# Three longer visits to the gate's projection in a chunk of the recurrence, in place of six

## The chip, the cores and the metric

The kernel runs on one core of a Trainium2 chip. The metric is the device time of one execution in microseconds (us), the median of some runs. A core has TensorE for matmuls (PE in the profile, and PEld for its weight loads), VectorE (DVE), ScalarE (ACT), GpSimd (POOL) and SyncE (SP), which here only issues transfers. Each engine works through its own instructions in the order in which they are written, and they meet at semaphores. TensorE writes into PSUM, eight banks from which VectorE and ScalarE carry the results away.

## The reference

One step of a decoder trunk with two layers over 1024 prompt tokens and 8 sample tokens: first an RWKV-7 layer with 32 heads of 64, then a latent attention layer. The change is in the RWKV-7 layer, in the recurrence over the prompt and the output that is made of it:

```
r, k, v, z = einsum('pbtd,pde->pbte', mixed, w_in)
...
def _wkv_step(S, inp):
    r, w, k, v, a, b = inp
    sa = einsum('bhvk,bhk->bhv', S, a)
    S = S * w[:, :, None, :] + sa[..., None] * b[:, :, None, :] + v[..., None] * k[:, :, None, :]
    return S, einsum('bhvk,bhk->bhv', S, r)
...
yn = ((y - mu) * rsqrt(var + GN_EPS)) * lnx_w + lnx_b      # per head
bonus = sum(rh * kh * r_k) * vh
out = ((yn + bonus) * silu(z)) @ w_out
```

The projection z is the gate's; nothing in the recurrence needs it.

## The kernel before, in words

The recurrence (`phase_r`, line 1208 on) takes the 1024 tokens in 32 chunks of 32, `for c in range(NC)`. The 32 heads are two groups g of 16. In a chunk each group goes through four small steps, and each is 16 to 32 short matmuls on TensorE into one PSUM bank and a copy out of it:

- `rh(c, g)` (line 1257): the right-hand side from the state; ScalarE copies it out as `rhs` (L1265).
- `sa(c, g)` (line 1267): the solve, with the inverse in tile U; ScalarE and VectorE each copy two quarters into the state tile st (L1276).
- `new_state(c, g)` (line 1278): the next state, named s in the trace; VectorE multiplies it with the decay into the other state tile in two instructions (L1289).
- `outs(c, g)` (line 1292): the chunk's output y, four copies by ScalarE (L1305).

rh needs the product of the state behind new_state of the chunk before, sa needs rhs, new_state needs the copies behind sa, and rh of the next chunk also needs the rows of v that `loadv` (line 1249) puts into the state tile; it is issued by SyncE and overwrites rows that outs(c - 1, 1) still reads. The loads of a later chunk's tiles X (xz) and U are issued beside it.

Between the small steps TensorE works on the gate's projection: `fill(w)` (line 1466) takes a number of steps of the generator zg, which is w times `rate` on average. A step is three matmuls of 128x344, named p in the trace; 333 steps are left when the loop starts, and `rate` (line 1461) spreads them over the chunks but for the last. Here this is called a visit. In the last chunk the output projection's generator opg takes their place.

The loop has six pieces a chunk, i = 0 to 5: rh of group 0; new_state of group 1 of the chunk before; sa of group 0 with outs of group 1 of the chunk before, and the loads; rh of group 1; new_state of group 0; sa of group 1 with outs of group 0. Behind each piece comes one step of the output block's generator ob, one step of the sample tokens' generator sg (a single-token recurrence on GpSimd and VectorE), and a visit with weight 0.8, or 1.4 behind the third and the sixth piece.

ob is `out_block(B)` (line 1432), started every four chunks for the outputs of the last four. It normalises them in two halves; each half is `out_half` (line 1315), with 18 steps, and the second half starts six steps after the first, so the block has 24 steps, as many as four chunks have pieces. Of a half, steps 0 and 1 and steps 7 and 8 are a reduce and its scale on VectorE, steps 9, 10, 14 and 15 are products on VectorE, steps 5 and 6 squares on ScalarE. Steps 16 and 17 each transpose half of the half on TensorE, four matmuls named ot (L1365), into the bank `tr`, of which there is one, and ScalarE copies it out as ozt (L1366). So step 17's transposes can start only when step 16's copy has ended. Step 17 also stores ozt.

Nothing plans the order: every engine gets its instructions in the order in which the loop and its generators issue them.

Of the kernel before, what the change touches and what calls it, by code (L numbers as in the profile page):

```python
# [31 lines left out]
NC = S // C  # L32
# [23 lines left out]
def tile_yoco(ctx, tc, A, O, dbg=None):  # L56
# [4 lines left out]
    def mm(out, lhsT, rhs, start, stop):  # L61
        PE.matmul(out, lhsT=lhsT, rhs=rhs, start=start, stop=stop)  # L62
# [97 lines left out]
    def run(g):  # L160
        for _ in g:
            pass

    def chain(*gs):
        for g in gs:
            yield from g
# [1041 lines left out]
    def phase_r(mh, ml, gC, bon, osT, SM, zg, zbank, zx):  # L1208

        with ExitStack() as px:  # L1210
# [9 lines left out]
            def psum(tag, name, bufs):  # L1220
                return ps.tile([P, 512], F32, tag=tag, name=name, bufs=bufs)

            def units(X):
                for s_ in range(2):
                    rows = slice(64 * s_, 64 * s_ + 64)
                    ACT.copy(X[rows, :, ts(2 * s_, 64)],
                             ident[rows, 64 * s_:64 * s_ + 64].unsqueeze(1).to_broadcast([64, 16, 64]))
# [3 lines left out]
            def load(c):  # L1231
                if c >= NC:
                    return
                X = XZ[c % NX]
                for s_ in range(2):
                    rows = slice(64 * s_, 64 * s_ + 64)
                    SY.dma_start(X[rows, :, 128 - 128 * s_:256 - 128 * s_], xs_d[s_, c].rearrange("r (a t) -> r a t", t=P))
                    (ACT if c > 2 else SY).dma_start(X[rows, :, 64 + 128 * s_:128 + 128 * s_], ra_d[:, rows, c].rearrange("a r t -> r a t"))
# [10 lines left out]
            def loadv(c):  # L1249
                if c < NC:  # L1250
                    SY.dma_start(ST[0][c % 2][96:128], v_d[0, ts(c, 32)])
                    SY.dma_start(ST[1][c % 2][32:64], v_d[1, ts(c, 32)])
# [4 lines left out]
            def rh(c, g):  # L1257
                X = XZ[c % NX]
                pr = psum("rh", f"rh{c}_{g}", 1)
                p3 = pr[:, 0:256].rearrange("p (q d) -> p q d", d=64)  # L1260
                for h in range(16 * g, 16 * g + 16):
                    j, q, s_ = h % 4, h // 4 - 4 * g, h % 2
                    mm(p3[ts(j, 32), q, :], X[:, h // 2, 128 * s_ + 96:128 * s_ + 128], ST[s_][c % 2][:, h // 2, :], True, True)
                t_ = rhs[g] = w1.tile([P, 4, 64], F32, tag=f"rh{g}", name=f"rhs{c}_{g}")
                ACT.copy(t_.rearrange("p q d -> p (q d)"), pr[:, 0:256])  # L1265

            def sa(c, g):
                U = Us[c]
                pa = [psum(f"sa{u}", f"sa{c}_{g}{u}", 1)[:, 0:256].rearrange("p (q d) -> p q d", d=64) for u in range(2)]
                for h in range(16 * g, 16 * g + 16):  # L1270
                    j, q = h % 4, h // 4 - 4 * g
                    mm(pa[j % 2][ts(j, 32), q, :], U[ts(j, 32), 4 * g + q, :], rhs[g][ts(j, 32), q, :], True, True)
                for j in range(4):
                    t_ = ST[0][c % 2][64:96] if j % 2 == 0 else ST[1][c % 2][0:32]
                    d = t_.rearrange("p (q two) d -> p q two d", two=2)[:, 4 * g:4 * g + 4, j // 2, :]
                    (V.tensor_copy if j % 2 else ACT.copy)(d, pa[j % 2][ts(j, 32)])  # L1276

            def new_state(c, g):

                X = XZ[c % NX]  # L1280
                p3 = psum("sy0", f"s{c}_{g}", 1).rearrange("p (q d) -> p q d", d=64)
                for q in range(8):
                    for s_ in range(2):
                        a = 8 * g + q
                        mm(p3[ts(s_, 64), q, :], X[:, a, 128 * s_:128 * s_ + 64], ST[s_][c % 2][:, a, :], True, True)
                qs = slice(8 * g, 8 * g + 8)
                for s_ in range(2):
                    rows = slice(64 * s_, 64 * s_ + 64)
                    V.tensor_tensor(ST[s_][1 - c % 2][rows, qs, :], p3[rows],  # L1289
                                    gC[rows, qs, c:c + 1].to_broadcast([64, 8, 64]), ALU.mult)  # L1290

            def outs(c, g):

                X = XZ[c % NX]
                B, ci = divmod(c, 4)
                if B not in ys:
                    ys[B] = w2.tile([P, 16, 2, 64], F32, tag="y", name=f"y{B}")
                p_ = psum("sy1", f"y{c}_{g}", 1)
                for m in range(4):
                    for j in range(4):  # L1300
                        a, s_ = 8 * g + 2 * j + m // 2, m % 2
                        mm(p_[ts(j, 32), ts(m, 64)], X[:, a, 128 * s_ + 64:128 * s_ + 96], ST[s_][c % 2][:, a, :], True, True)
                for j in range(4):
                    a = 8 * g + 2 * j
                    ACT.copy(ys[B][ts(ci, 32), a:a + 2].rearrange("p a s d -> p (a s d)"), p_[ts(j, 32), 0:256])  # L1305
# [126 lines left out]
            def out_block(B, lag=6):  # L1432
                a, b = out_half(B, 0), out_half(B, 1)
                n = 0
                while a is not None or b is not None:
                    if a is not None and next(a, end) is end:
                        a = None
                    if n >= lag and b is not None and next(b, end) is end:
                        b = None
                    n += 1  # L1440
                    yield
# [5 lines left out]
            sg = sample_step(sp, lambda n: psum("tr", n, 1), osT, SM)  # L1447
# [16 lines left out]
            ob = chain()  # L1464

            def fill(w):
                nonlocal due
                due += w * rate
                while due >= 1.0:
                    next(zg, None)  # L1470
                    due -= 1.0

            for c in range(NC):
                for i in range(6):
                    if i == 0:
                        rh(c, 0)
                    elif i == 1:
                        if c:
                            new_state(c - 1, 1)
                            if c % 4 == 0:  # L1480
                                run(ob)
                                ob = out_block(c // 4 - 1)
                        if c == NC - 1:
                            run(sg)
                            run(zg)
                            rx.close()
                            zx.close()
                            opg = op_open()
                    elif i == 2:
                        sa(c, 0)  # L1490
                        if c:
                            outs(c - 1, 1)
                        loadv(c + 1)
                        load(c + 2)
                        loadu(c + 2)
                        if c == 2:
                            SY.dma_start(lnw, A["a_lnx_w"].to_broadcast([P, DI]))
                        if c == 0:
                            for X in XZ[1:]:
                                units(X)  # L1500
                    elif i == 3:
                        rh(c, 1)
                    elif i == 4:
                        new_state(c, 0)
                    else:
                        sa(c, 1)
                        outs(c, 0)
                    next(ob, None)
                    next(sg, None)
                    fill(1.4 if i % 3 == 2 else 0.8)  # L1510
                    if c == NC - 1 and i in (1, 5):
                        next(opg)
            new_state(NC - 1, 1)
            outs(NC - 1, 1)
# [14 lines left out]
            ob = out_last(NC // 4 - 1)  # L1529
# [44 lines left out]
    def op_open():  # L1574
        rp = rsx.enter_context(tc.tile_pool(name="rsp", bufs=1, side="right", reuse_waits="tile"))
        mid["RS"] = rp.tile([P, T], F32, name="RS")

        for nm, sh in (("cks", [P, 2, NB]), ("kps", [64, NB]), ("ckn", [NB, KVL]),
                       ("qsp", [64, HB, NB]), ("zsb", [P, HB, NB])):
            mid[nm] = rp.tile(sh, F32, name=nm)  # L1580
        mid["idx"] = rp.tile([P, NB, 8], I32, name="idx")
        wx = mid["wx"] = ExitStack()
        wA = wx.enter_context(tc.tile_pool(name="wA", bufs=1, side="right", reuse_waits="tile"))
        mid["op"] = a_out(wx, wA)
        return mid["op"]
# [1187 lines left out]
```

## Time and profile before

| | us |
|---|---|
| median of 3 runs | 2931.27 (2929.74 to 2937.22) |
| the profiled execution, its own time | 2943.64 |
| its span, first to last instruction | 2941.9 |
| TensorE busy in the span | 2696.3 (92%) |
| VectorE busy | 1672.7 (57%) |
| ScalarE busy | 1361.2 (46%) |
| GpSimd busy | 1430.5 (49%) |

The busy shares are means over the whole program. The recurrence is the stretch from about 990 to 1484 us of the span. A row of the timeline gives the start and the length of an instruction or of several merged ones (xcount); in the brackets at its end stands how long the engine was idle before it and what ended that. "issue" means that nothing in the profile shows what it waited for. PEclk is the granted clock of TensorE as a share of its full 2.4 GHz. A matmul's end is modelled, so matmuls that follow each other overlap in the rows; the distance of two starts is what they cost.

### The profile page before, as it was taken

To read this page: it belongs to the slowest core of one execution; us is meant where nothing else is said; L and a number is where in the kernel's file an instruction comes from. 1 tells how busy PE (TensorE), PEld (TensorE's weight loads), DVE (VectorE), ACT (ScalarE), POOL (GpSimd) and SP (SyncE) were. 2 spreads that over 40 slices of the span, in tenths; PEclk is the share of its full clock that TensorE was granted. 3 is DMA by queue.
4 is the path that set the end of the run, shared out by engine and by line. 5 is a ranking of instruction groups with operands and counts; after the bars stand their busy time and mean duration, and the time that the engine had idled before them with its cause. 6 is when DMAs were issued, how large, how long until landed. Compare 5 with 4: busy or idle time off the path is not lost.

```text
span 2941.9 us, 64866 instructions
## 1 busy us (share of the span) xinstructions
PE 2696.3 (92%) x26386; PEld 2418.5 (82%) x26386; DVE 1672.7 (57%) x2952; ACT 1361.2 (46%) x2886; POOL 1430.5 (49%) x1385
## 2 busy tenths in 40 slices
PE   7999998878786788888879999999999999899998
PEld 7999997766675677767769989999999999666897
DVE  7232117989797756666574144127777777533414
ACT  7232226767675444445454335225555555333423
POOL 3322121699999566663245455313444433475342
PEclk9999999989898899999989999999999999999999
DMA  4332334667677899999777552322111111586525
GB/s 157 120 126 76 96 88 113 162 145 174 155 162 190 206 223 218 227 227 210 175 228 225 173 123 78 107 83 83 54 56 54 56 52 55 157 274 201 179 90 187
DMA packets 567501, 423.80 MB, mean 144 GB/s; under 512 B 176260, under 2 KB 515649, under 8 KB 567074
## 3 DMA queue, kind: packets, MB, share of 16 engines
q1 hardware_dynamic: 473954, 336.06, 42.5%
q10 hardware_dynamic: 79648, 38.42, 4.9%
q0 software_dynamic: 13600, 45.16, 4.9%
q8 instruction: 208, 3.41, 0.5%
q14 instruction: 91, 0.75, 0.1%
HBM read 281.69 MB, written 133.35 MB: 141 GB/s over the span
## 4 chain that ended last, share of the span: by engine, by line
PE 57%; POOL 7%; DVE 7%; DMA 5%; issue 4%; ACT 3%; SPq 1%; ACTq 0%; DVEq 0%; POOLq 0%
PE p L62 8%; PE zb L62 6%; PE sc L62 6%; PE bo L62 5%; PE wop L62 4%; PE o L62 4%; POOL Xt L1081 2%; POOL X L1083 2%; PE s L62 2%; PE q L62 2%; PE pt L2156 2%; PE v L62 2%; PE k L62 1%; PE pt L2575 1%; PE bt L62 1%
## 5 line engine op out<-in xcount | busy, mean ns | idle before, releaser
L76 POOL TENSOR_TENSOR wl<-wr,wh 128x1024 fp32r<-128x1024 f32 x32 | 84.3, 2654 | 288.0 <-ACT wh L71 269.5
L1081 POOL TENSOR_TENSOR Xt<-N,X 128x31 f32<-128x31 f32 (+15 forms) x217 | 187.0, 862 | 27.2 <-DMA N<-n_d 11.0
L1083 POOL TENSOR_TENSOR X<-X,Xt 128x31 f32<-128x31 f32 (+15 forms) x217 | 183.8, 847 | 17.0
L71 ACT CAST pth<-pt 128x256 fp32r<-128x256 f32 (+1 forms) x320 | 108.2, 355 | 128.8 <-DVE ptl L76 74.8
L1289 DVE TENSOR_TENSOR st<-s,gC 64x512 f32<-64x512 f32 x128 | 88.2, 689 | 131.6 <-PE s L62 129.2
L62 PE MATMUL p<-mh,w3h 128*128 128x344 f32 x384 | 149.6, 390 | 6.2 <-issue 5.0
L76 DVE TENSOR_TENSOR ptl<-pt,pth 128x256 fp32r<-128x256 f32 (+1 forms) x320 | 120.9, 391 | 27.0 <-ACT pth L71 25.0
L62 PE MATMUL p<-ml,w3h 128*128 128x344 f32 x384 | 130.8, 341 | 5.1 <-issue 2.9
L62 PE MATMUL p<-mh,w1h 128*128 128x344 f32 x360 | 134.9, 375 | 0.0
L62 PE MATMUL p<-mh,w3l 128*128 128x344 f32 x384 | 127.1, 337 | 3.7 <-issue 3.7
L62 PE MATMUL r<-mh,wh 128*128 128x344 f32 x384 | 124.7, 325 | 4.6 <-ACT tf L483 4.6
L62 PE MATMUL r<-mh,wl 128*128 128x344 f32 x384 | 124.1, 323 | 0.0
L62 PE MATMUL r<-ml,wh 128*128 128x344 f32 x384 | 123.9, 323 | 0.0
L2139 ACT ACTIVATE pr<-sc,mx 128x128 f32<-128x128 f32 (+7 forms) x128 | 95.4, 745 | 53.1 <-DVE mx L2136 51.6
L62 PE MATMUL p<-mh,w1l 128*128 128x344 f32 x360 | 119.9, 333 | 0.0
L62 PE MATMUL p<-ml,w1h 128*128 128x344 f32 x360 | 119.8, 333 | 0.0
L2136 DVE TENSOR_REDUCE mx<-sc 128x1 f32<-128x128 f32 (+7 forms) x128 | 96.7, 755 | 3.2
L1305 ACT COPY y<-y 32x256 f32<-32x256 f32 x256 | 93.2, 364 | 10.7 <-PE y L62 7.1
L1276 ACT COPY st<-sa 32x256 f32<-32x256 f32 x128 | 46.4, 362 | 111.1 <-PE sa L62 100.7
L1950 DVE TENSOR_TENSOR zbr<-zb,RS 128x384 f32<-128x384 f32 (+1 forms) x48 | 24.6, 515 | 126.1 <-PE zb L62 123.8
L62 PEld LDWEIGHTS s<-st,xz 128*64 128x64 f32 x2048 | 72.6, 148 | 27.9 <-issue 20.9
L2041 POOL TENSOR_TENSOR qp<-qp,rope 128x256 f32<-128x256 f32 (+1 forms) x30 | 22.4, 747 | 145.8 <-DMA qsw<-qp 122.4
(1237 smaller groups left out, 9944.9 us busy)
## 6 DMA issues: line engine op xcount, KB each, us to landing
xs_d<-XS SPq DMA_DIRECT2D x64, 512.0 KB, 5.9
xz<-xs_d SPq DMA_DIRECT2D x64, 512.0 KB, 9.0
wr<-in_a_w_in_dram SPq DMA_DIRECT2D x17, 1024.0 KB, 6.1
ra_d<-RA SPq DMA_DIRECT2D x32, 512.0 KB, 7.3
xz<-ra_d ACTq DMA_DIRECT2D x58, 256.0 KB, 7.4
rT_d<-rr ACTq DMA_DIRECT2D x16, 516.0 KB, 2.6
R<-rT_d SPq DMA_DIRECT2D x16, 516.0 KB, 3.5
w3r<-in_a_w_in_dram SPq DMA_DIRECT2D x16, 512.0 KB, 6.2
```

Source lines behind the costliest of these rows:

```text
L62: PE.matmul(out, lhsT=lhsT, rhs=rhs, start=start, stop=stop)
L71: ACT.copy(out, in_)
L76: (eng or V).tensor_tensor(out, in_, hi_.bitcast(F32), ALU.subtract)
L1081: eng.tensor_tensor(t3, N_[:, s_:s_ + 1, s_ + 1:].to_broadcast([P, a, b]), X_[:, r0:r1, s_:s_ + 1].to_broadcast([P, a, b]), ALU.mult)
L1083: eng.tensor_tensor(X_[:, r0:r1, s_ + 1:], X_[:, r0:r1, s_ + 1:], t3, ALU.add)
L1276: (V.tensor_copy if j % 2 else ACT.copy)(d, pa[j % 2][ts(j, 32)])
L1289: V.tensor_tensor(ST[s_][1 - c % 2][rows, qs, :], p3[rows], gC[rows, qs, c:c + 1].to_broadcast([64, 8, 64]), ALU.mult)
L1305: ACT.copy(ys[B][ts(ci, 32), a:a + 2].rearrange("p a s d -> p (a s d)"), p_[ts(j, 32), 0:256])
L2136: V.tensor_reduce(mx, sc[:, :W], AX.X, ALU.max, negate=True)
L2139: ACT.activation(pr[:, :W], sc[:, :W], AF.Exp, bias=mx, accum_out=sm)
L2156: PE.transpose(pt[:, ts(q, P)], pr[:, ts(g + q, P)], ident)
L2575: PE.transpose(p_[:, ts(r, P)], pg[:, r, ts(c, P)], ident)
```

## The change

The loop has three blocks a chunk in place of six pieces. Block 0: rh of group 0, then new_state of group 1 of the chunk before. Block 1: sa of group 0, rh of group 1, outs of group 1 of the chunk before, and the loads. Block 2: new_state of group 0, sa of group 1, outs of group 0. Behind each block come two steps of ob and two of sg, taken in turn, and then one visit with weight 2.0. The weights of a chunk add up to 6 as before, and no instruction is added or left out.

```diff
             for c in range(NC):
-                for i in range(6):
+                for i in range(3):
                     if i == 0:
                         rh(c, 0)
-                    elif i == 1:
                         if c:
                             new_state(c - 1, 1)
                             if c % 4 == 0:
                                 run(ob)
                                 ob = out_block(c // 4 - 1)
...
-                    elif i == 2:
+                    elif i == 1:
                         sa(c, 0)
+                        rh(c, 1)
                         if c:
                             outs(c - 1, 1)
                         loadv(c + 1)
...
-                    elif i == 3:
-                        rh(c, 1)
-                    elif i == 4:
+                    else:
                         new_state(c, 0)
-                    else:
                         sa(c, 1)
                         outs(c, 0)
-                    next(ob, None)
-                    next(sg, None)
-                    fill(1.4 if i % 3 == 2 else 0.8)
-                    if c == NC - 1 and i in (1, 5):
+                    for _ in range(2):
+                        next(ob, None)
+                        next(sg, None)
+                    fill(2.0)
+                    if c == NC - 1 and i in (0, 2):
                         next(opg)
```

TensorE's order in the middle of a chunk, before: the last matmul of rh of group 1, a visit, new_state of group 0 (s), a visit, the first matmul of sa of group 1. A row is the line, the operation, the written tile and what it reads; p is the projection, and its operands mh and ml are the input's high and low parts.

```order
L62 MATMUL rh_1_12321<-st_0_9721,xz_9718 32x64
L62 MATMUL p_6_2_12311<-mh_98,w3h_0_11588 128x344
L62 MATMUL p_6_2_12311<-ml_106,w3h_0_11588 128x344
L62 MATMUL p_6_2_12311<-mh_98,w3l_0_11644 128x344
L62 MATMUL s_0_12349<-st_0_9719,xz_9718 64x64
...
L62 MATMUL p_6_2_12311<-mh_99,w3h_1_11832 128x344
...
L62 MATMUL p_6_2_12311<-mh_100,w3l_1_11834 128x344
L62 MATMUL sa_10_12382<-rhs_1_12338,U_11823 32x64
```

The same place in the change: rh of group 1 with outs (y) of the chunk before behind it, one visit of nine p, and then s and sa without a visit between them.

```order
L62 MATMUL rh_1_12278<-st_0_9721,xz_9718 32x64
L62 MATMUL y_1_12297<-st_1_9720,xz_9717 32x64 x4
...
L62 MATMUL p_6_2_12252<-mh_96,w3h_0_11610 128x344
...
L62 MATMUL p_6_2_12252<-mh_98,w3l_0_11703 128x344
L62 MATMUL s_0_12352<-st_0_9719,xz_9718 64x64
...
L62 MATMUL s_0_12352<-st_0_9721,xz_9718 64x64
L62 MATMUL sa_10_12371<-rhs_1_12295,U_11847 32x64
```

What moved: the two short visits around s are one longer one ahead of it.

TensorE's order at the end of such a chunk, where ob makes the transposes of an output half (ot_00 and ot_01), before:

```order
L62 MATMUL y_0_12404<-st_0_9721,xz_9718 32x64 x4
L1365 MATMUL ot_00_12429<-ctab,y_10932 128x128 x4
L62 MATMUL p_6_2_12311<-mh_101,w3h_1_11832 128x344
...
L62 MATMUL p_6_2_12311<-mh_102,w3l_1_11834 128x344
L62 MATMUL rh_0_12446<-st_1_9720,xz_9727 32x64
...
L1365 MATMUL ot_01_12465<-ctab,y_10932 128x128 x4
L62 MATMUL p_7_0_12477<-mh_95,w3h_0_12136 128x344
```

And in the change:

```order
L62 MATMUL y_0_12393<-st_0_9721,xz_9718 32x64 x4
L1365 MATMUL ot_00_12418<-ctab,y_10926 128x128 x4
L1365 MATMUL ot_01_12426<-ctab,y_10926 128x128 x4
L62 MATMUL p_6_2_12252<-mh_99,w3h_1_11853 128x344
L62 MATMUL p_6_2_12252<-ml_107,w3h_1_11853 128x344
```

What moved: the second group of transposes stands directly behind the first; this is so for all 14 pairs of the loop.

ScalarE's order at the same place, before: two copies of sa, four of y, the first ozt, a copy of the projection (zrow), rhs, the second ozt.

```order
L1276 COPY st_0_9719<-sa_10_12382 32x4x64 x2
L1305 COPY y_11916<-y_0_12404 32x256 x4
L1366 COPY ozt_12428<-ot_00_12429 128x512
L772 COPY zrow_2_12443<-p_6_2_12311 128x344
L773 DMA zT_d<-zrow_2_12443 128x344
L1265 COPY rhs_0_12463<-rh_0_12446 128x256
L1366 COPY ozt_12428<-ot_01_12465 128x512
```

And in the change:

```order
L1276 COPY st_0_9719<-sa_10_12371 32x4x64 x2
L1305 COPY y_11907<-y_0_12393 32x256 x4
L1366 COPY ozt_12417<-ot_00_12418 128x512
L1366 COPY ozt_12417<-ot_01_12426 128x512
L71 CAST w3h_1_12436<-w3r_11941 128x512
L772 COPY zrow_2_12452<-p_6_2_12252 128x344
```

What moved: the second ozt follows the first; what stands ahead of the first is the same.

## Rows read from the trace of the kernel before

**Rows 1.** The page's first line.

```profile
span 2941.9 us, 64866 instructions
```

**Rows 2.** Busy time of the recurrence: PE, PEld, DVE, ACT, POOL, clock, DMA, GB/s.

```profile
990.00:1484.00 494.00, 424.81 (x9224) 351.94 (x9225) 306.01 (x538) 232.53 (x589) 246.43 (x179) 0.92 0.90 209
```

**Rows 3.** Timeline of TensorE in one chunk: start, length, instruction.

```profile
1130.21 0.32 PE L62 MATMUL p<-mh,w3l 128*128 128x344 f32 x1
1130.46 0.65 PE L62 MATMUL rh<-st,xz 128*32 128x64 f32 x32
1131.04 0.43 PE L62 MATMUL p<-mh,w3h 128*128 128x344 f32 x1
1131.30 0.32 PE L62 MATMUL p<-ml,w3h 128*128 128x344 f32 x1
1131.46 0.32 PE L62 MATMUL p<-mh,w3l 128*128 128x344 f32 x1
...
1132.19 1.15 PE L62 MATMUL s<-st,xz 128*64 128x64 f32 x32
1133.27 0.42 PE L62 MATMUL p<-mh,w3h 128*128 128x344 f32 x1
...
1133.94 0.65 PE L62 MATMUL sa<-rhs,U 32*32 32x64 f32 x32
1134.52 0.65 PE L62 MATMUL y<-st,xz 128*32 128x64 f32 x32
...
1136.73 0.65 PE L62 MATMUL rh<-st,xz 128*32 128x64 f32 x32
```

**Rows 4.** TensorE's waits, 1050 to 1480 us: total, times, longest.

```profile
PE p L62 <- issue: 11.5, 6, 2.9
...
PE sa L62 <- issue: 6.0, 6, 1.8
...
PE ot L1365 <- ACT ozt L1366: 3.0, 4, 2.3
```

**Rows 5.** Timeline around a first group of transposes, ScalarE and TensorE.

```profile
1304.36 0.74 ACT L1276 COPY st<-sa 32x256 f32<-32x256 f32 x2 [2.48 <-PE sa L62]
...
1304.83 0.66 PE L1365 MATMUL ot<-ctab,y 128*128 128x128 f32 x4
1305.11 1.51 ACT L1305 COPY y<-y 32x256 f32<-32x256 f32 x4
...
1305.24 0.40 PE L62 MATMUL p<-mh,w3h 128*128 128x344 f32 x1
...
1306.64 0.59 ACT L1366 COPY ozt<-ot 128x512 f32<-128x512 f32 x1
```

**Rows 6.** Timeline of TensorE around its longest wait for ozt.

```profile
1364.73 0.40 PE L62 MATMUL p<-mh,w3h 128*128 128x344 f32 x1
...
1369.23 0.66 PE L1365 MATMUL ot<-ctab,y 128*128 128x128 f32 x4 [2.25 <-ACT ozt L1366]
```

**Rows 7.** Busy time of the stretch behind that wait; columns as in rows 2.

```profile
1370.50:1373.50 3.00, 3.00 (x36) 2.88 (x35) 1.15 (x2) 0.53 (x2) 0.00 (x0) 0.50 0.80 218
```

**Rows 8.** DMA queue of code in the recurrence: packets, MB, share.

```profile
q8 instruction: 72, 1.18, 1.1%
```

**Rows 9.** VectorE's instructions by line in the recurrence: busy, mean ns, idle before.

```profile
L1289 DVE TENSOR_TENSOR st<-s,gC 64x512 f32<-64x512 f32 x126 | 86.8, 689 | 129.4 <-PE s L62 126.9
...
L1340 DVE TENSOR_REDUCE rs<-sq 128x8 f32<-128x512 f32 x28 | 18.9, 674 | 0.2
L1341 DVE TENSOR_SCALAR rs<-rs 128x8 f32<-128x8 f32 x28 | 14.5, 517 | 1.0
```

**Rows 10.** Timeline of SyncE: issues of the loads of v.

```profile
1129.43 0.43 SPq L1251 DMA_DIRECT2D st<-v_d  x1
...
1130.04 0.32 SPq L1252 DMA_DIRECT2D st<-v_d  x1
```

**Rows 11.** Tile st: the loads of v, from issue to landing.

```profile
DMA to landing us min/median/max: 2.5/4.6/6.2
```

## The prediction

> **What bounds the kernel now.** I read the views in this order: the page's span, the busy time of the recurrence as one stretch, TensorE's instructions of one chunk in order of time, and who waited for whom. The profiled execution took 2943.64 us, its span is 2941.9 us [rows 1], and the median of the three runs shown is 2931.27 us; the sum below is a difference made in the profiled execution, and I add it to the median. The change touches only the recurrence, from about 990 to 1484 us: 494.0 us for 32 chunks, 15.4 us each, of which TensorE is busy 424.8 at a mean granted clock of 0.92, VectorE 306.0 and ScalarE 232.5 [rows 2]. So TensorE is what this stretch waits for, and an edit is worth what it does to TensorE's order.
>
> That order alternates a small step (rh, s, sa or y: 32 short matmuls) or two with a visit to the gate's projection (p) [rows 3]. Two p matmuls inside a visit start 0.16 us apart (1131.30, 1131.46). The first p of a visit needs 0.26 until the second (1131.04, 1131.30), and the last p needs 0.25 until the small step starts (1130.21, 1130.46). A small step rh lasts 0.58 to the p behind it (1130.46 to 1131.04), and sa lasts 0.58 to the small step behind it (1133.94 to 1134.52). The rest of the 494 us is mostly waits that the trace calls issue, which no semaphore ends: five rows of TensorE's waits, from p with 6 waits of 11.5 us to sa with 6 of 6.0, together 28 waits and 42.3 us [rows 4]. Its waits for ozt are small, 3.0 us [rows 4].
>
> **Term 1, fewer visits.** A visit that goes gives back 0.25 - 0.16 at its end and 0.26 - 0.16 at its start, 0.19 us; the p matmuls stay the same in number, and a small step costs the same before another one as before p. A chunk has three visits instead of six, in the 31 chunks in which p is left: 93 x 0.19 = -17.7 us. In the new order rh stands directly before y, both with tiles of 128*32; no row shows that passage, and if it cost nothing beyond the matmuls it would save at most another 0.1 a chunk, so the term lies between -17.7 and -21. Where TensorE waits anyway it is worth less (term 4).
>
> **Term 2, the two transpose groups of an output half.** The output block's steps come in twos now. Its steps 16 and 17, and 22 and 23, both fall behind the third block of a chunk, and these are the transposes ot of one half: two groups of four into the one bank tr, each emptied by ScalarE's ozt copy. Before, a visit and the step rh stood between them; now the second group is TensorE's very next instruction, as the order of the change shows, and everything behind it, the next visit first, waits with it. When does ozt end? ScalarE works in order: at 1304.36 two sa copies of 0.74, at 1305.11 four y copies of 1.51, and only at 1306.64 ozt, which takes 0.59 and ends at 1307.23; the transposes had started at 1304.83, and TensorE could go on at 1305.24 [rows 5]. From there to the end of ozt it would stand still for 1.99 us. There are 14 such pairs (seven blocks of four chunks, two halves), 27.9 us, less the 3.0 that TensorE waits for ozt today: +24.9 us. From below, if ScalarE were free at once, a pair would cost one ozt, 14 x 0.59 - 3.0 = +5.3; from above, if each were as late as the latest of today (p went on at 1364.73 behind the first group, and the second started at 1369.23, behind a wait of 2.25 [rows 6]), 14 x 4.50 - 3.0 = +60. I take the ordinary case of rows 5, since the order of ScalarE's copies ahead of ozt stays.
>
> The Trainium skill bears on this place: Perfetto Trace Analysis, "Optimizing Tensor Performance", says that independent matmul groups should rotate through different banks so that the emptying of one overlaps the matmuls of the next. The change goes against it; taken as the price of one emptying alone, the rule would make the term +5.3 and the sum about -2. The trace shows more, since four y copies stand ahead of ozt. This is rival B.
>
> **Term 3, the clock behind such a wait.** Behind that wait of 2.25 us the granted clock was 0.50 from 1370.5 to 1373.5, that is 1.2 GHz of 2.4, with TensorE busy all the time [rows 7]. Three microseconds at half clock lose about 1.5. If each of the 14 pairs brought that it would be 21 us, if none 0. The new waits are a little shorter than that one, and I take three of them, +5.
>
> **Term 4, waits for code.** The queue q8 brought 72 packets, 1.18 MB, in the recurrence [rows 8], about 16 KB each; 28 issue waits of 1.5 us on average stand against these 72. That the waits belong to the packets is inference. If so, two effects oppose: a wait of 2 us at a pair gives a packet time to come, 14 x 28/72 x 1.5 = -8; and where a packet is waited for, the time that fewer visits save is only waited longer, 17.7 x 28/72 = +7. I take 0; the ends are -21 (each pair replaces one such wait) and +7.
>
> The Trainium skill, Runtime: NRT & Kernel Launch, "Instruction fetch mechanics", says that the sequencer streams code in blocks of 16 KiB and that crossing into a new block is mostly hidden. The packet size agrees, the 42.3 us speak against hidden; by the rule this term is 0 too, without its ends.
>
> **Term 5, VectorE in bursts.** The state product behind s is two instructions of 0.69, and a reduce with its scale takes 0.67 + 0.52 [rows 9]. Steps 6 and 7 of the output block are now issued together, three such reduces, 3.6 us, behind the product of a first block (1.4) and ahead of the sa copies that the s of the third block needs. A visit takes 1.9 (10.7 p on average at 0.16, and 0.19). From the end of s in the first block to the end of sa in the second TensorE takes 1.9 + 0.6 = 2.5, so the sa copies start 2.5 late; with 0.8 for them (ScalarE's two take 0.74) VectorE ends 3.3 behind sa, and TensorE wants them after rh, y and a visit, 3.1 behind it. So this is covered but for 0.2, and anything else in VectorE's queue (a weight product or a reduce of the sample, some 0.7 each) comes on top. Seven times 0 to 2 us: I take +3, ends 0 and +14.
>
> **Term 6, the loads of v.** SyncE issues them when y of the chunk before is done, at 1129.43 and 1130.04 [rows 10]; they land 2.5 to 6.2 us later, median 4.6 [rows 11], and the rh that needs them started at 1136.73 [rows 3], 7.3 after the first issue. The new order has rh ahead of y, and only two visits, s (1.1), sa and y behind it: 2 x 1.9 + 1.1 + 1.2 = 6.1 us. Counted from there and with the second issue 0.6 later, the median lands at 5.2 and the longest at 6.8. So most stay hidden, late ones cost up to 0.7, and two chunks in four have a pair's wait as more room: +2, ends 0 and 31 x 0.7 = +22. The other loads of SyncE are issued in the same place, two chunks ahead, and keep more than a chunk of room: 0.
>
> **Sum.** -17.7 + 24.9 + 5 + 0 + 3 + 2 = +17.2: 2931.27 + 17 = 2948 us, +0.6%. Less than 0.3% (8.8 us) either way counts as no change, about what a measurement of this kernel can tell.
>
> **Rivals.**
> A, faster: the pairs' waits fall where TensorE would have stood anyway. If 12 of the 14 replace an issue wait of 1.5 us, and the room they give covers terms 3, 5 and 6, then -17.7 + 24.9 - 18 = -11, 2920 us. For it: issue waits are the largest of all. Against it: 28 in 72 packets, so a pair meets one in 39 of 100. It decides from 11 of the 14 on. Chance 0.13.
> B, no change: ScalarE reaches ozt sooner than in rows 5. With one ozt a pair, -17.7 + 5.3 + 10 = -2; with half of the ordinary price, -17.7 + 12.5 + 10 = +5: 2929 to 2936 us, 2932 in the middle. Against it: nothing that stands ahead of ozt leaves its place. Chance 0.24.
> C, slower still: with rh ahead of y the load of v sets the pace in 20 chunks (+14), and the clock falls behind 11 pairs (+17): -17.7 + 24.9 + 17 + 14 = +38, 2969 us. For it: the slowest landing of today would be late by itself. Against it: the median of 4.6. Chance 0.18.
> My forecast has 0.45. Faster by over 0.3% has 0.13, within it 0.24, slower 0.63. The range leaves out the far part of A and the upper end of C: 2924 to 2968; the forecast's own is 2940 to 2957.
>
> **What would show it.** In the changed profile: the second ot group waits for ozt 14 times, about 1.8 us each, in place of 3.0 us in all; 9 or 12 p stand in a row, with three passages fewer a chunk; issue waits stay near 42 us; a few waits of rh for v of under 1 us; the s of a third block rarely waits for VectorE. I am wrong if the pairs cost under 1 us each, if issue waits fall by over 15 us, or if most chunks wait for v.

## The result, and the profile after

The changed kernel took 2957.34 us (median of 5 runs, 2954.32 to 2962.28), the kernel before 2937.22 on the same chip (2929.74 to 2940.57): a ratio of 1.0074, 95% interval 1.0057 to 1.0092, or 20.1 us more. The profiled execution after took 2957.34 us with a span of 2955.5, and that of before 2943.64, so the two traces differ by 13.7 us only (the execution of before was 6.4 above the median). Nearly all of that lies in the recurrence. From its first rh to the matmul behind its last chunk the trace of before shows 496.8 us and that of after 510.0; the rest of the span is 2445.1 and 2445.5.

The busy row of the recurrence, columns as in [rows 2]: TensorE is busy 14 us less than in [rows 2] in a stretch that is 14 us longer.

```profile
990.00:1498.00 508.00, 410.67 (x9243) 358.85 (x9244) 319.80 (x537) 235.97 (x594) 246.91 (x178) 0.91 0.88 205
```

TensorE's waits from 1050 to 1495 us, where [rows 4] has 1050 to 1480 (total, times, longest):

```profile
PE ot L1365 <- ACT ozt L1366: 23.6, 13, 2.4
PE s L62 <- issue: 19.1, 8, 4.8
PE rh L62 <- issue: 13.6, 6, 5.6
PE y L62 <- issue: 7.5, 8, 2.9
PE sa L62 <- issue: 4.8, 5, 2.0
PE s L62 <- ACT st L1276: 2.9, 1, 2.9
PE rh L62 <- DVE st L1289: 2.8, 6, 0.7
PE p L62 <- issue: 1.3, 1, 1.3
```

The wait for ozt, 3.0 us before, is now the largest row. The five issue rows are again 28 waits, 46.3 us in place of 42.3. A wait of rh for the load of v, 2.8 us before in this stretch, is not there any more.

One pair of transpose groups, in order of time (start, length, engine, instruction, idle before it); it answers to [rows 5]:

```profile
1234.77 0.74 ACT L1276 COPY st<-sa 32x256 f32<-32x256 f32 x2 [0.98 <-PE sa L62]
...
1235.23 0.66 PE L1365 MATMUL ot<-ctab,y 128*128 128x128 f32 x4
1235.52 1.48 ACT L1305 COPY y<-y 32x256 f32<-32x256 f32 x4
...
1237.03 0.58 ACT L1366 COPY ozt<-ot 128x512 f32<-128x512 f32 x1
...
1237.66 0.66 PE L1365 MATMUL ot<-ctab,y 128*128 128x128 f32 x4 [1.77 <-ACT ozt L1366]
1238.07 0.41 PE L62 MATMUL p<-mh,w3h 128*128 128x344 f32 x1
```

ScalarE has the same queue as before: two sa copies, four y copies, then ozt. The second group starts 2.43 us behind the first; without a wait the next instruction starts 0.41 behind a group (1237.66 to 1238.07), so a pair costs 2.02. The bracket's 1.77 is less, because it counts from the modelled end of the first group.

The passages between steps, TensorE alone, in one chunk of after:

```profile
1216.96 0.65 PE L62 MATMUL rh<-st,xz 128*32 128x64 f32 x32
1217.43 0.63 PE L62 MATMUL y<-st,xz 128*32 128x64 f32 x32
1217.99 0.42 PE L62 MATMUL p<-mh,w3h 128*128 128x344 f32 x1
...
1219.84 0.32 PE L62 MATMUL p<-mh,w3l 128*128 128x344 f32 x1
1220.08 1.15 PE L62 MATMUL s<-st,xz 128*64 128x64 f32 x32
1221.16 0.65 PE L62 MATMUL sa<-rhs,U 32*32 32x64 f32 x32
```

A visit now holds 9 or 12 p (12 here), and the passage out of it costs 0.24 (1219.84 to 1220.08), as in [rows 3]. In the passage that no row of before showed, rh straight to y, rh lasts 0.47, not 0.58, so that passage costs 0.11 less than the others.

The clock behind two of the pairs, columns as in [rows 7]:

```profile
1376.70:1380.10 3.40, 3.40 (x15) 3.39 (x13) 0.00 (x0) 1.03 (x2) 0.06 (x1) 0.50 0.57 156
1482.50:1485.90 3.40, 3.40 (x14) 3.40 (x14) 0.00 (x0) 0.58 (x1) 3.40 (x2) 0.50 0.31 94
```

The second groups of these pairs started at 1376.30 and 1482.36. Six of the 14 pairs have such a stretch that begins within a microsecond of their second group. Others went away in exchange, so that over the chunks 3 to 30 the time at 0.50 (1.2 GHz) is 58.0 us after and 47.8 before. A second execution of each kernel has 64.9 (e5) and 27.3 (e12).

### The profile page after: what moved, and what is told of

Same layout as the page of the kernel before. It is cut to its first block, busy times and chain, and to the rows that moved or that the text cites. A ratio compares the mean times of both kernels' runs of the same rounds, so it can differ in the third digit from the quotient of the medians.

```text
span 2955.5 us, 64902 instructions
## 1 busy us (share of the span) xinstructions
PE 2687.3 (91%) x26386; PEld 2430.6 (82%) x26386; DVE 1683.0 (57%) x2952; ACT 1362.8 (46%) x2886; POOL 1432.2 (48%) x1385
## 4 chain that ended last, share of the span: by engine, by line
PE 55%; DVE 8%; POOL 7%; DMA 5%; issue 5%; ACT 3%; SPq 1%; ACTq 0%; DVEq 0%; POOLq 0%
PE p L62 7%; PE sc L62 6%; PE zb L62 6%; PE bo L62 5%; PE wop L62 4%; PE o L62 4%; POOL X L1083 2%; PE s L62 2%; POOL Xt L1081 2%; PE q L62 2%; PE pt L2154 2%; PE v L62 2%; PE k L62 1%; PE bt L62 1%; PE pt L2573 1%
## 5 line engine op out<-in xcount | busy, mean ns | idle before, releaser
L62 PE MATMUL s<-st,xz 128*64 128x64 f32 x2048 | 82.7, 235 | 22.0 <-issue 19.1
L1276 ACT COPY st<-sa 32x256 f32<-32x256 f32 x128 | 46.3, 362 | 116.7 <-PE sa L62 109.4
```

## The experiments

Twelve runs on three chips. The time of before differs between chips (2973.0 us beside e1, e2, e4 and e6, 2940.0 beside e5, e7, e8 and e9, 2977.5 beside e10, e12, e13 and e14), so each kernel is compared by its ratio to before on its own chip. The rows of the table can't be compared so: with all its bytes, before has a trace in the result and one in e12, and none beside the other eight runs. Rows of waits are from 1050 to 1480 us where nothing else is said.

To compare the traces I split the time of the chunks 3 to 30 in the same way for each kernel: TensorE's gaps over 0.25 us by what ended them, half of the time that the clock stood at 0.50, and the remainder, which is TensorE's own time (matmuls at full clock and passages). The half is an estimate, the rest is summed from the rows. "VectorE" includes waits of s, rh and ot for it. One execution each; between two executions of one kernel the total moves by up to 7 us.

| kernel | chunks 3 to 30 | TensorE's own | issue | ozt | VectorE | other waits | half of low clock |
|---|---|---|---|---|---|---|---|
| before | 424.2 | 348.8 | 42.1 | 2.5 | 0.5 | 6.4 | 23.9 |
| before again (e12) | 418.4 | 353.9 | 41.7 | 0.3 | 1.9 | 7.0 | 13.6 |
| after | 435.4 | 332.6 | 43.8 | 23.6 | 2.8 | 3.6 | 29.0 |
| after again (e5) | 442.5 | 330.5 | 49.2 | 23.1 | 2.9 | 4.3 | 32.5 |
| e1 second bank | 434.7 | 329.3 | 48.0 | 0 | 11.9 | 4.5 | 41.0 |
| e14 second bank again | 432.4 | 330.9 | 51.2 | 0 | 15.7 | 5.5 | 29.0 |
| e13 no second vb | 423.1 | 334.4 | 49.4 | 0 | 7.7 | 5.9 | 25.6 |
| e2 pair in before | 443.3 | 349.8 | 32.7 | 21.6 | 7.2 | 0 | 32.0 |
| e4 steps apart | 413.3 | 339.4 | 39.5 | 0 | 13.6 | 3.9 | 17.0 |
| e6 after, few bytes | 381.0 | 332.3 | 4.1 | 25.4 | 6.4 | 0.8 | 12.0 |
| e7 before, few bytes | 356.5 | 350.5 | 0 | 2.7 | 3.3 | 0 | 0 |
| e8 steps apart, few bytes | 363.1 | 338.5 | 7.0 | 0.8 | 11.4 | 0.3 | 5.1 |
| e9 second bank, few bytes | 356.8 | 336.2 | 4.9 | 0 | 10.2 | 2.1 | 3.4 |

**e1: the pair without its wait.** After, with the second transpose group in another PSUM bank.

```
-                    p_ = psum("tr", f"ot{B}_{hf}{g}", 1)
+                    p_ = psum("sa0" if g else "tr", f"ot{B}_{hf}{g}", 1)
```

> The changed kernel, with the second transpose group of an output half in bank sa0 instead of tr; order, visits and bursts of steps stay. Pair theory (the loss is the second group's wait for ozt, the gain is the fewer visits): TensorE's waits of ot for ozt fall from 23.6 us to under 3, the time falls by 20 to 26 us, to about 0.2% above or below the kernel before (ratio 0.998 to 1.001). Burst theory (the loss comes from the steps being issued in twos, so that VectorE and ScalarE are late for the recurrence): the waits for ozt go, but the time stays within 6 us of the changed kernel (ratio 1.005 to 1.009). Cover theory (a wait at a pair only stands in for an issue wait): issue waits grow from 46 to 60 us or more, and the time falls by less than 10 us.

2991.9 us, ratio 1.0060 [1.0043, 1.0076]. The waits for ozt are gone, and the time is not: it gives back 0.14% of the change's 0.74%, which is within the intervals, as the burst theory had it. Its waits, TensorE and then VectorE:

```profile
PE s L62 <- issue: 17.6, 7, 4.1
PE rh L62 <- issue: 17.1, 10, 6.5
PE ot L1365 <- DVE y L1357: 7.5, 6, 3.4
...
PE rh L62 <- DVE st L1289: 5.5, 13, 1.2
```

```profile
DVE y L1357 <- POOL vb L1351: 25.3, 5, 8.9
```

New waits for VectorE stand in their place: the transposes for the y that VectorE adds up last, and rh for the state products queued on it. VectorE in turn waits 25.3 us for GpSimd's product with vb. So the price of the pairs was not simply on top.

**e2: the pair alone.** Before, with both transpose groups in one step and nothing else changed.

```
                     ACT.copy(oz[:, 4 * g:4 * g + 4, :].rearrange(...), p_)
-                    if g == 0:
-                        yield
+                yield
```

> The kernel before with its six pieces and six visits, where step 16 of an output half makes both transpose groups, so that they stand next to each other; step 17 only stores. Pair theory: 13 to 14 waits for ozt of about 1.8 us, and a time 20 to 28 us above the kernel before (ratio 1.007 to 1.010). Burst theory: no burst was added, so under 5 us (ratio below 1.002). Cover theory: the waits appear, but issue waits fall by as much, and the ratio stays below 1.003.

2992.67 us, ratio 1.0056 [1.0038, 1.0073], +16.6 us by the ratio (the two medians differ by 19.7), less than the pair theory's 1.007 to 1.010. The trace is of the slowest of the six executions, 3002.61 us.

```profile
PE ot L1365 <- ACT ozt L1366: 19.8, 10, 3.3
PE s L62 <- issue: 9.9, 5, 2.9
...
PE ot L1365 <- DVE y L1347: 4.3, 1, 4.3
```

By the ratios the pair alone makes three quarters of the loss, though the intervals of the two overlap. In this order a part of it seems to fall where TensorE would have stood anyway: the issue waits are 32.7 us against 42.1, the only order with all the bytes in which they fell by more than 3 us.

**e4: the fewer visits alone.** Before, with a visit behind every second piece and the six pieces kept for the steps of the output block and the sample, so that no two transposes stand together.

```
                         sa(c, 0)
+                    elif i == 3:
+                        rh(c, 1)
                         if c:
                             outs(c - 1, 1)
...
-                    elif i == 3:
-                        rh(c, 1)
...
-                    fill(1.4 if i % 3 == 2 else 0.8)
+                    if i % 2:
+                        fill(2.0)
```

> Three visits a chunk as in the change, but the steps of the output block and of the sample tokens stand one by one behind each of the six pieces, as before; so a visit and rh lie between the two transpose groups. Pair theory with 0.19 us per visit: no waits for ozt, no bursts, and 15 to 20 us less than the kernel before (ratio 0.993 to 0.996). If fewer visits are worth nothing because TensorE then only waits longer for code: ratio 0.999 to 1.002, with issue waits up by 15 us or more. Burst theory: ratio 0.999 or below, with clearly less time than in the run with the second bank.

2978.7 us, ratio 1.0018 [1.0004, 1.0031]. No gain. TensorE's own time is 9 us below that of before (14 below e12), and the waits for VectorE are 13.6 us. Yet this recurrence, 488.5 us, is shorter than both traces of before (496.8 and 489.9), which are from other chips, while on its own chip the kernel is the slower one; so what takes up the 9 to 14 us here can't be read from these traces.

```profile
PE s L62 <- DVE st L1276: 5.0, 5, 2.0
...
PE rh L62 <- DVE rs L1345: 2.1, 2, 1.7
PE rh L62 <- DVE ms L1100: 1.9, 1, 1.9
PE rh L62 <- DVE st L1276: 1.8, 3, 1.1
PE rh L62 <- DVE st L1289: 1.8, 5, 0.4
PE ot L1365 <- DVE y L1357: 1.5, 3, 1.0
```

e1, on the same chip, differs from e4 by the steps in twos and the second bank, and its ratio is higher by 0.42%, with the intervals apart. So the twos cost time without any wait at a pair.

**e6: after, with less traffic beside the code.** From the fourth chunk on, the loads of X bring 8 rows of 64.

```
-                    rows = slice(64 * s_, 64 * s_ + 64)
+                    n = 64 if c < 3 else 8
+                    rows = slice(64 * s_, 64 * s_ + n)
```

(and `:n` in the source of both loads.)

> The changed kernel; from chunk 3 on the loads of the tiles X carry 8 of 64 rows, so the recurrence's results are not the reference's, and the number of instructions is the same. If the issue waits are code packets that come late behind data in the DMA engines: the issue waits between 1050 us and the end of the recurrence fall from 46 us to under 20, and the time by 25 us or more. If they are not (they depend on how fast TensorE uses up its code alone): issue waits stay above 35 us, and the time falls by less than 10 us. The waits for ozt stay at 14 of 1.8 us either way.

2936.78 us, ratio 0.9875 [0.9858, 0.9891]. From 990 to 1484 us there are as many code packets as in [rows 8] (74), and the issue waits are nearly gone; the wait for ozt stays whole (TensorE, 1050 to 1430 us). (An edit that adds lines moves the line numbers behind it: L1366 here is L1365 above.)

```profile
PE ot L1366 <- ACT ozt L1367: 25.4, 13, 3.0
PE rh L62 <- DVE st L1290: 4.5, 10, 0.8
PE rh L62 <- issue: 3.0, 2, 2.8
...
PE y L62 <- issue: 1.3, 1, 1.3
```

**e5: after unaltered, once more.**

> The changed kernel unaltered, beside the kernels below on one chip. Every theory: 0.5 to 0.9% above the kernel before, 14 waits of about 1.8 us of ot for ozt.

2962.81 us, ratio 1.0077 [1.0051, 1.0104]. The difference comes again. Whether this is the chip of the result isn't on record.

**e7, e8, e9: before, e4 and e1 with the small loads of e6.** The edits are those shown, taken together.

> The kernel before; from chunk 3 on the loads of the tiles X carry 8 of 64 rows (the recurrence's results are not the reference's). Issue waits fall from 42 us to under 10, as they did in the changed kernel with few bytes. Cover theory (what the change saves or costs on TensorE is partly exchanged for code waits, which come late behind data): without code waits the change is worth its bare terms, fewer visits -17 and pairs +25, so this kernel is 5 to 12 us under the changed kernel with few bytes (ratio 0.981 to 0.986, against 0.9875 there). Data theory (the recurrence is bound by the transfers of X, and TensorE's order matters only beside that): with the transfers gone the two differ by under 4 us.

> Three visits with the steps of the output block and the sample tokens apart, and few bytes for X from chunk 3 on as above. Cover theory: with the code waits gone the 0.19 us of a visit show, 13 to 18 us below the kernel before with few bytes (ratio lower by 0.0045 to 0.006). VectorE theory (fewer visits leave the state product too little time, and TensorE waits for VectorE instead): less than 6 us below it, and waits for DVE of 10 us or more in the recurrence.

> The changed kernel with the second transpose group in bank sa0, and few bytes for X from chunk 3 on as above. Cover theory: with the code waits gone the pairs' full price shows, 18 to 25 us below the changed kernel with few bytes (ratio 0.979 to 0.982). VectorE theory: the waits move to the last product of the output block (ot behind y of VectorE) and to the state product, 10 us or more of them, and the time falls by under 12 us (ratio above 0.9835).

e7 2875.05 us, ratio 0.9782 [0.976, 0.9804]; e8 2877.75, 0.9798 [0.9771, 0.9825]; e9 2876.0, 0.9786 [0.9763, 0.9808]. The three don't differ within their intervals. The waits of e7, and then the larger ones of e9, TensorE, 1050 to 1410 us:

```profile
PE s L62 <- DVE st L1277: 2.9, 4, 1.7
PE ot L1366 <- ACT ozt L1367: 2.7, 5, 1.1
...
PE p L62 <- issue: 0.2, 1, 0.2
```

```profile
PE rh L62 <- DVE st L1290: 7.7, 17, 0.9
PE y L62 <- issue: 5.3, 2, 2.9
PE s L62 <- DVE st L1277: 2.7, 2, 2.2
PE rh L62 <- issue: 2.7, 2, 2.5
```

Two things follow. With few bytes a pair's wait costs its full price: e6 and e9 differ by 0.9% of before, 26 us (two chips, so by their ratios), for 25.4 us of waits. And three visits in place of six gain nothing even here. TensorE's own time falls by 12 to 14 us (e7 to e8 and e9, one chip, one trace each), and waits for VectorE (+7 to +8), for code (+5 to +7) and the low clock (+3 to +5) take it all. So the expectation of e7 failed: the whole change costs 0.9% with few bytes (e7 to e6), some 27 us and not 5 to 12, which is about the pairs' price without the -17 that was set against it. The twos without the pairs' wait cost nothing here (e9 against e8).

**e14, e13, e12: e1 once more, e1 without the second load of vb, and before, on a third chip.** The edit of e13 beside e1's; its second output half multiplies the first half's rows of v:

```
-                vb = vbs.pop((B, hf)).rearrange("p s q d -> p q s d")
+                vbt = vbs.pop((B, hf))
+                vb = vbt.rearrange("p s q d -> p q s d")
...
-                    loadvb(B, 1)
+                    vbs[B, 1] = vbt
```

> The changed kernel with the second transpose group in bank sa0, once more, beside the kernels below on one chip. If the first run of it was right: ratio 1.004 to 1.008, so that freeing the pairs gives back under 10 us while all bytes are loaded; if that run was a chance of its chip, ratio 0.998 to 1.002 as the pair theory has it.

> The changed kernel with the second transpose group in bank sa0, and without the load of v rows (vb) for the second half of an output block; that half uses the first half's rows, so its bonus is not the reference's. vb theory (with the steps in twos this load is issued only one visit ahead of GpSimd's product, VectorE waits for that product with the recurrence's copies queued behind it): VectorE's waits for vb fall from 25 us to under 8, and the time is 8 to 15 us below the run with the second bank alone. Code theory (what is freed turns into waits for code packets): VectorE's waits fall but the time stays within 5 us of it, with issue waits above 45 us.

> The kernel before, unaltered, for a second profile of it. Every theory: its recurrence takes 487 to 497 us, with 35 to 45 us of issue waits and under 5 us of waits for ozt.

e14 2990.27 us, ratio 1.0043 [1.0026, 1.0061]; e13 2977.56, 1.0006 [0.9990, 1.0022]; e12, run once, 2971.19, which is 6.3 under that chip's median for the same kernel. VectorE's wait for vb in e14 with TensorE's behind it, and then VectorE's in e13:

```profile
DVE y L1357 <- POOL vb L1351: 26.8, 5, 10.1
PE ot L1365 <- DVE y L1357: 10.2, 8, 4.0
```

```profile
DVE y L1358 <- POOL vb L1352: 2.2, 3, 1.1
```

With that load gone the waits of ot for y are gone too, and 12.7 us of time with them (the two traces differ by 8.7 us in the recurrence and by 4.8 outside it). So once the pair's wait is taken away, the load of vb comes next on the path. Even without both, the order with three visits only reaches the time of before. The e13 kernel moves fewer bytes than before as well, so it shows no gain of the visits either.

**e10: one load of X in place of two.** Before, with both parts of X side by side in the scratch memory, one load for each head group from there by SyncE, and X's columns in another order for it. The smaller stores that this needs lie in the stage before the recurrence.

```
-                    SY.dma_start(X[rows, :, 128 - 128 * s_:256 - 128 * s_], xs_d[s_, c].rearrange("r (a t) -> r a t", t=P))
-                    (ACT if c > 2 else SY).dma_start(X[rows, :, 64 + 128 * s_:128 + 128 * s_], ra_d[:, rows, c].rearrange("a r t -> r a t"))
+                    SY.dma_start(X[rows, :, 64 - 64 * s_:256 - 64 * s_], xr_d[s_, c].rearrange("r (a u) -> r a u", u=192))
```

> The kernel before, with the two scratch tensors from which a chunk's tile X is loaded laid out as one, so that a chunk has two loads with pieces of 768 B in place of four with pieces of 512 and 256 B; the bytes loaded are the same, and ScalarE issues none of them. The stores into it before the recurrence are in smaller pieces. Data theory (code packets and loads come late because of the many small packets in the DMA engines): issue waits fall from 42 us to under 25 and the recurrence by 15 us or more; the time falls by 10 to 25 us unless the stores cost it again. Byte theory (the bytes, not the packets, fill the DMA engines): issue waits stay above 35 us, and the time moves by less than 8 us either way, or rises where the stores are late.

2998.87 us, ratio 1.0078 [1.0058, 1.0098]: slower, and most of it in the recurrence (512.1 us, e12 489.9: 22.2 of the 26.9 us by which the two traces differ). The packets of the recurrence fall by a third, the bytes don't (e10, then e12):

```profile
DMA packets 127582, 103.08 MB, mean 201 GB/s; under 512 B 15809, under 2 KB 117062, under 8 KB 127366
```

```profile
DMA packets 192087, 103.67 MB, mean 212 GB/s; under 512 B 80341, under 2 KB 181437, under 8 KB 191869
```

Issue waits of the chunks 3 to 30 stay: 38.5 us, 41.5 with the one that ends where chunk 3 begins, against 41.7 in e12. What is new is v (e10, TensorE, 1050 to 1490 us):

```profile
PE rh L62 <- DMA st<-v_d: 12.9, 7, 3.6
PE ot L1370 <- DVE y L1362: 7.5, 5, 2.7
```

SyncE's queue now carries all of X beside v; that v stands behind it there is inference. As a try to lower the waits for code by fewer packets, it failed.

## Why the prediction was right

The number was right (+17 forecast, +20 measured), and so were the place and the length of the wait that it rests on most. That the rest of the sum closed was in part luck: its gain (term 1) does not show as a gain in any run, and its largest cost (term 2) hid another cost that stood in no term. In absolute time, 2957 lies at the upper end of the forecast's own 2940 to 2957; 6 us of that are before's, whose median of five runs is 2937. The terms, against the traces of before and after:

- **Term 2, +24.9, is the largest cost, and its price is right.** A pair costs 2.02 us where 1.99 was forecast, from the ordinary case of [rows 5], in which nothing ahead of ozt leaves its place. The row counts 23.6 us in 13 waits; a 14th stands at the end of the recurrence, behind the window. e2 has the pair alone at +16.6 us, e6 and e9 have it at 26. Taken out of the changed kernel with all its bytes (e1, e14), it gives back 4 to 10 only.
- **Term 3, +5:** 10.2 us more at half clock, about 5 lost, behind six pairs where three were taken. It isn't firm: the two traces of before alone differ by 20.5 us at half clock.
- **Term 4, 0:** 28 issue waits before and after, 42.3 and 46.3 us. Of the two effects that it sets against each other, e2 shows the cover (42 to 33). The longer waits are there in e1, e13 and e14, which have no pairs' waits and fewer visits (48 to 51), but not in e4, which has fewer visits and no pairs' waits too (39.5); so the fewer visits alone don't make them.
- **Term 5, +3:** right in size, by another path. No s waits for VectorE's sa copies, as the term had it; rh waits six times, 2.8 us, for VectorE's state product, and s waits once, 2.9, for ScalarE's sa copies. And it stays so small only while the pairs' waits are there: without them the waits for VectorE are 8 to 16 us (e1, e4, e13, e14), and in e1 and e14 the largest part is the y that is late behind vb, a load that no term has. That the pairs' waits are what gives VectorE this time is inferred from these runs.
- **Term 6, +2:** a miss, small. From chunk 3 on no rh waits for v after, and the 2.8 us of before went away (e5 has 2.1, e4 3.5). In the first three chunks the waits for v rose from 11.5 to 15.8 us, but these chunks take 58.9 us against 59.5.
- **Term 1, -17.7, is right as TensorE's time and wrong as a gain.** TensorE's own time falls by 16 us from before to after (84 visits fewer in the 28 chunks, 0.19 each; 0.25 of each pair's 2.02 is counted in it too, so the visits save rather more). But taken by itself (e4) the step gives +0.18%, not -0.6%, and nothing with few bytes either (e8). The saving is not free time on the path: with few bytes VectorE, the code and the clock take what TensorE gives up; with all the bytes what takes it is open. The sum adds the terms as if each stood alone. It came out because the pairs' waits and the waits for VectorE cover one another in the changed kernel: the pairs alone cost 0.56% (e2), the change without them still costs 0.43 to 0.60% (e14, e1), and both together 0.74%.

The sum for the changed kernel, from the table: own time -16.2, ozt +21.1, VectorE +2.3, other waits -2.8, issue +1.7, clock +5.1, together +11.2 of the 13.2 that the two recurrences differ; e5 in place of after gives +18.3, with issue at +7.1 and the clock at +8.6; with e12 in place of before the two are +17.0 and +24.1. So one trace of each fixes the sum to some 7 us only. The remaining 2 us of the 13.2 are the last chunk's, with the 14th pair (+2.7), less 0.7 in the first three.

Rival A fell: the issue waits didn't go down, so on balance the pairs replaced none of them here. Rival B fell with the 2.02 us of a pair. The Trainium skill, Perfetto Trace Analysis, "Optimizing Tensor Performance", has the rule behind it, to rotate independent groups through banks: the trace agrees that one bank makes a wait, but it lasts through ScalarE's y copies and the copy of the bank, 1.77 us, not through the 0.58 of that copy alone, and the rotation is worth 4 to 10 us (e1, e14) while VectorE is late behind it and 26 with few bytes (e9). Rival C fell: from chunk 3 on v was not late, and the clock fell behind six pairs, not eleven.

What stays open: why three orders of steps (e7, e8, e9) come to the same time with few bytes, within 0.2%. VectorE is busy 316 of some 430 us there and is what TensorE waits for, which speaks for the chain from TensorE over VectorE's copies and state products and back. No run here made that chain shorter, so it isn't shown.

## What to carry to other kernels

Ask of every passage or visit that is saved on the busiest engine which other engine used that time, and take the saving away alone before it is counted in a sum. When steps of a generator are issued in twos, look for the two that share a bank or a buffer: the second waits for whatever stands ahead of the emptying on its engine, here six copies and not one. A wait that is taken away shows the next one behind it, so a fix of one line is worth what the second-latest releaser leaves of it. For the same reason two costs of one change can hide one another, and a sum of terms can come out for the wrong reason: take each out by itself.

## What the runs showed of the hardware

TensorE's issue waits are waits for code, and they go with the data. That they belong to the code packets was inference in the prediction; the packets' times in the traces show it. In the chunks 3 to 30 the issue waits over 0.25 us end 1.2 to 1.7 us behind the end of a code packet: 27 of 27 in before, 22 of 22 in after, 30 of 30 in e12, and 246 of 255 in the ten traces with all the loads of X. Of times spread evenly over the same stretches 8% lie so, and of the waits that something else ended 2 of 186.

The 72 or 73 code packets of a recurrence cost 33 to 51 us of issue waits beside some 103 MB of data. With few bytes e7 has the same number of packets, 65 MB and one wait of 0.2 us, and e6, e8 and e9 have 4 to 7 us. A code packet itself takes 1.2 us on average in before and in e7 alike, so the data don't lengthen its own transfer; what they delay is not shown. The queue's row of after, and then that of e7 in its recurrence (packets, MB, share), and all packets of before and of e7:

```profile
q8 instruction: 73, 1.20, 1.0%
```

```profile
q8 instruction: 72, 1.18, 1.2%
```

```profile
DMA packets 192225, 103.34 MB, mean 209 GB/s; under 512 B 80340, under 2 KB 181763, under 8 KB 192009
```

```profile
DMA packets 88960, 64.57 MB, mean 151 GB/s; under 512 B 28363, under 2 KB 78283, under 8 KB 88743
```

The Trainium skill, Runtime: NRT & Kernel Launch, "Instruction fetch mechanics", calls the crossing into a new block of code mostly hidden. That holds in e7 and not with the full loads. With the waits the low clock went too: between 1040 and 1410 us e7's granted clock was never below full, while before spent 48 us at half in the chunks 3 to 30. The recurrence of e7 took 427.2 us, that of before 496.8, and on e7's chip the kernel fell from 2940.0 to 2875.1, so the traffic of the loads of X is worth more than any order of the steps tried here. One rival is untested: with few bytes TensorE also multiplies other values, since most of X stays as it was, and whether that bears on the clock no run shows. By e10 it isn't the number of packets: a third fewer, with the same bytes, left the issue waits about where they were.
